# Keeping every engine's instructions in the order of the kernel's own plan

## The chip, the cores and the metric

The kernel runs on one core of a Trainium2 chip. The metric is the device time of one execution in microseconds (us); lower is better. A core has five engines with a queue of instructions each: TensorE (PE, with its weight loads shown apart as PEld), VectorE (DVE), ScalarE (ACT), GpSimd (POOL) and SyncE (SP), which here issues all transfers (DMAs). An engine starts its instructions in the order of its queue; an instruction whose operands aren't there yet waits, and so does all that stands behind it.

## The reference

One step of a decoder layer for 16 meta tokens, a prompt of 256 and 8 samples of 4 new tokens, 304 rows (T) in all, each 2048 wide, in fp32:

```python
xn = rms_norm(x, norm_mix)
z = xn @ w_in                                  # 2048 -> 7456 columns
o_a, S_a = rwkv7_mixer(z[..., :RWKV_COLS], ...)    # 16 heads of 64: a recurrence over tokens
o_b, S_b = retention_mixer(z[..., RWKV_COLS:], ...) # 4 heads of 256: rotary, masked scores, state
h = x + concatenate([o_a, o_b]) @ w_out
hn = rms_norm(h, norm_ffn)
h = h + (silu(hn @ w_gate) * (hn @ w_up)) @ w_down  # 2048 -> 5632 -> 2048
y = rms_norm(h, norm_final)
```

The kernel returns y, and the new states of both kinds of heads.

## The kernel before

**The main stream.** All large products have the activations transposed, 128 channels on the partitions and up to 304 tokens in the free dimension. Weights come from HBM in blocks of 128 x 1024 fp32 (`load`, buffers "wr", four of them). `halve` (L540) splits 512 columns into a rounded half "wh", by a cast on ACT (L545), and a rest "wl", by a subtraction on DVE (L546); four buffers of each. For every 128 x 128 piece TensorE then runs three matmuls (L584 to L586): rounded weights by rounded activations (xh), by the activations' rest (xl), and weights' rest by xh. 512 columns are thus a step of 12 matmuls. `main` (L552) goes through all jobs in a fixed sequence: 59 column tiles of the input projection ("in"), 32 of the output projection in two halves ("out"), then the FFN in groups of four gate and up tiles and 16 short "down" jobs. Results are summed in PSUM in two "acc" buffers, and each job's sum is taken out by an evacuation on DVE or ACT. At the start of each 512-column step `main` calls the load of a block up to 4096 columns ahead (L577) and the split of the weights that TensorE reads two steps later (L579, L580). In the first 16 pieces it also converts the input x to xh and xl as it arrives (`convert`, L576 and L582).

**The head streams.** Everything else runs beside it as generators: eight pairs of RWKV heads (`pair`, L817, with `inverse` at L1000, `sample`, and `units` at L1080), four retention heads (`ret`, L1291), small low-rank weights (`lora_weights`, L784), evacuations, norms. They use small fp32 matmuls in other PSUM tiles ("mm"), with DVE, ACT and GpSimd in between. `inverse` has a loop of 15 steps, each a shuffle on DVE (L1017), a product and a sum on GpSimd; later it copies products to a tile yy on ACT (L1064) between two sets of matmuls. `units` goes through five time units, each with four matmuls and an update of the state on DVE (L1114). `pair` begins with a scaled copy kk on ACT (L841). A pair may begin while the one before is still at work, so two pairs and a retention head are usually under way.

**The order.** The kernel plans its own order. Each engine handle is wrapped in `Timed`, and each call is first booked with estimated durations in the class `Plan`: for DVE 60 + 1.05 ns for each element of a row, for ACT 190 + 0.84, for GpSimd 100 + 2.2, and a latency (L336). TensorE is booked in `array`, SP not at all. `run` (L380) asks after each three matmuls of the main stream whether a generator is due on the estimated clock of TensorE; if so it lets it run to its next `yield`, and sets its next due time to the end of what it has just called, or 300 ns later if nothing was booked (L376). So the calls come in an order in which, by these estimates, everything is ready when its turn comes. The temporary tiles of the streams all lie in one large tile, "arena", whose places are assigned in a first pass of the same plan (the draft), and may be used again soon after.

The tile framework then makes five queues of these calls. [...]

Of the kernel before, what the change touches and what calls it, by code (L numbers as in the profile page):

```python
# [288 lines left out]
class Timed:  # L289


    def __init__(self, plan, eng, name):
        self._plan, self._eng, self._name = plan, eng, name

    def __getattr__(self, what):
        f = getattr(self._eng, what)

        def call(*a, **k):
            self._plan.book(self._name, what, a, k)
            return f(*a, **k)  # L300

        return call


class Plan:
# [1 line left out]

    def __init__(self, nc, rooms, draft):  # L310
        self.rooms, self.draft, self.count = rooms, draft, 0
        self.clock = dict(PE=0.0, DVE=0.0, ACT=0.0, POOL=0.0)
        self.ready = self.end = 0.0
        self.mode, self.parts, self.empty, self.begun = None, {}, 0.0, 0.0
        self.streams, self.made = [], 0
        self.pe = Timed(self, nc.tensor, "PE")
        self.dve = Timed(self, nc.vector, "DVE")
        self.act = Timed(self, nc.scalar, "ACT")
        self.pool = Timed(self, nc.gpsimd, "POOL")
        self.sp = Timed(self, nc.sync, "SP")  # L320
# [151 lines left out]
class Step:  # L472


    def __init__(self, tc, I, O, ctx, rooms, draft):
        self.tc, self.nc, self.I, self.O = tc, tc.nc, I, O
        self.rooms, self.draft = rooms, draft
        pool = lambda n, b, **k: ctx.enter_context(tc.tile_pool(name=n, bufs=b, **k))
        self.cp = pool("const", 1)
        self.wp = pool("weights", 1)  # L480
        self.mp = pool("scratch", 1)
        self.ap_ = pool("acc", ACC, space=bass.MemoryType.PSUM)
        self.pp = pool("psum", 8 - ACC, space=bass.MemoryType.PSUM)
        self.n = 0
        self.plan = pl = Plan(self.nc, rooms, draft)
        self.sp = pl.sp
        if not draft:
            self.arena = {dt: self.mp.tile([P, r.size], dt, tag=f"arena_{dt}", name=f"arena_{dt}")
                          for dt, r in rooms.items()}
        self.pe, self.dve, self.act, self.pool = pl.pe, pl.dve, pl.act, pl.pool  # L490
        self.outs = []
        self.live = 0
        self.done = set()
# [1182 lines left out]
```

## Time and profile before

| what | value |
|---|---|
| median of three runs (lowest, highest) | 1583.23 us (1579.57, 1583.24) |
| profiled execution | 1582.62 us |
| its span, first to last instruction | 1580.8 us |
| mean granted TensorE clock | 0.992 |
| busy, share of the span: PE / DVE / ACT / POOL | 98% / 71% / 53% / 12% |
| DMA, mean over the span | 160 GB/s, 252.50 MB |

Rows of the profile name an instruction by engine, operation and tiles: `mm<-arena_dt.float` is a matmul of a head stream, `acc<-xh,wh` one of the main stream, `arena_dt.float<-mm` takes a result of the first out of PSUM. All calls pass through the helper, so every row has line L300; the shape and the tiles tell which one it is. In the timeline the brackets give the idle time of the engine before an instruction, and what ended it. TensorE's matmuls overlap: one of 288 columns is shown with some 295 ns and starts about 133 ns after the one before.

### The profile page before, as it was taken

What the parts mean: (1) busy time and instruction counts of PE and PEld (TensorE: products, weight loads), DVE (VectorE), ACT (ScalarE), POOL (GpSimd) and SP (SyncE); (2) the same over time, 40 slices, a digit from 0 to 9 for tenths busy, and PEclk for the clock granted to TensorE, in tenths of its full rate; (3) what the DMA queues carried; (4) which work ended last, traced back from release to release, by engine and by line L of the source; (5) the groups of instructions that cost most, each with busy time, mean ns of one, the idle gap of its engine ahead of it and who ended that gap; (6) DMA issues with size and microseconds to landing.
All of it is one profiled execution on the core that took longest, in us unless ns stands there. A gap on an engine that the chain in (4) does not pass through costs nothing.

```text
span 1580.8 us, 30987 instructions
## 1 busy us (share of the span) xinstructions
PE 1544.1 (98%) x11388; PEld 1510.5 (96%) x11388; DVE 1125.7 (71%) x2590; ACT 842.7 (53%) x1795; POOL 182.5 (12%) x567
## 2 busy tenths in 40 slices
PE   9999999999999999999999999999999999999997
PEld 8989899998988989999999999999999999999997
DVE  7888789887997877776565656666666666565657
ACT  6756777577766556365444444444444444444445
POOL 1463314513143000000000000000000000000000
PEclk9999999999999999999999999999999999999999
DMA  7543344334544547755555555555555555555553
GB/s 280 152 126 108 102 121 138 118 102 126 181 131 139 168 161 231 241 162 160 166 167 165 169 163 171 162 171 161 169 165 166 168 163 171 162 172 162 169 163 114
DMA packets 77000, 252.50 MB, mean 160 GB/s; under 512 B 9392, under 2 KB 14640, under 8 KB 76848
## 3 DMA queue, kind: packets, MB, share of 16 engines
q1 hardware_dynamic: 76848, 250.52, 51.0%
q8 instruction: 90, 1.47, 0.4%
q14 instruction: 62, 0.51, 0.1%
HBM read 236.21 MB, written 14.28 MB: 158 GB/s over the span
## 4 chain that ended last, share of the span: by engine, by line
PE 68%; ACT 1%; DVE 1%; DMA 0%; issue 0%; POOL 0%; DVEq 0%; ACTq 0%; POOLq 0%
PE acc L300 64%; PE mm L300 4%; ACT arena_dt.float L300 1%; DVE arena_dt.float L300 1%; DMA arena_dt.float<-s0r 0%; DVE wl L300 0%; ACT wh L300 0%; ACT arena_dt.float32r L300 0%; POOL arena_dt.float L300 0%; DVEq L1672 0%; DVE arena_dt.float32r L300 0%; ACTq L300 0%; DVEq L300 0%; POOLq L300 0%
## 5 line engine op out<-in xcount | busy, mean ns | idle before, releaser
L300 ACT CAST wh<-wr 128x512 fp32r<-128x512 f32 x826 | 509.5, 619 | 577.4 <-PE acc L300 537.8
L300 PE MATMUL acc<-xh,wh 128*128 128x288 f32 (+2 forms) x2592 | 791.8, 305 | 0.5 <-ACT wh L300 0.3
L300 DVE TENSOR_TENSOR wl<-wr,wh 128x512 fp32r<-128x512 f32 x826 | 571.3, 693 | 282.2 <-ACT wh L300 259.9
L300 PE MATMUL acc<-xh,wl 128*128 128x288 f32 (+2 forms) x2592 | 771.3, 298 | 0.7 <-DVE wl L300 0.7
L300 PE MATMUL acc<-xl,wh 128*128 128x288 f32 (+2 forms) x2592 | 768.1, 296 | 0.0
L300 PEld LDWEIGHTS acc<-xh,wh 128*128 128x128 f32 x2592 | 488.3, 188 | 6.4 <-issue 2.7
L300 PEld LDWEIGHTS acc<-xl,wh 128*128 128x128 f32 x2592 | 487.5, 188 | 4.6 <-issue 1.4
L300 PEld LDWEIGHTS acc<-xh,wl 128*128 128x128 f32 x2592 | 486.9, 188 | 1.7 <-DVE wl L300 1.2
L300 PE MATMUL acc<-arena_dt.float32r,wh 128*128 128x288 f32 x1408 | 280.3, 295 | 0.0
L300 PEld LDWEIGHTS acc<-arena_dt.float32r,wh 128*128 128x128 f32 x1408 | 225.4, 188 | 0.3 <-ACT arena_dt.float32r L300 0.2
L300 PE MATMUL acc<-arena_dt.float32r,wl 128*128 128x288 f32 x704 | 206.8, 294 | 0.0
L300 PE MATMUL mm<-arena_dt.float 128*128 128x128 f32 (+8 forms) x1072 | 171.9, 320 | 19.3 <-DVE arena_dt.float L300 10.6
L300 PEld LDWEIGHTS mm<-arena_dt.float 128*128 128x128 f32 (+1 forms) x1072 | 140.2, 185 | 36.9 <-issue 10.5
L300 DVE TENSOR_TENSOR arena_dt.float<-arena_dt.float 128x288 f32<-128x288 f32 (+10 forms) x483 | 157.3, 351 | 11.1 <-ACT arena_dt.float L300 4.4
L300 DVE TENSOR_TENSOR arena_dt.float<-arena_dt.float,acc 128x288 f32<-128x288 f32 x208 | 94.3, 454 | 64.3 <-PE acc L300 63.8
L300 PEld LDWEIGHTS acc<-arena_dt.float32r,wl 128*128 128x128 f32 x704 | 132.8, 189 | 0.0
L300 ACT COPY arena_dt.float<-mm 64x64 f32<-64x64 f32 (+9 forms) x330 | 92.4, 287 | 53.0 <-PE mm L300 48.1
L300 ACT ACTIVATE arena_dt.float<-arena_dt.float 128x288 f32<-128x288 f32 (+6 forms) x200 | 85.3, 432 | 33.8 <-DVE arena_dt.float L300 28.0
L300 DVE TENSOR_TENSOR arena_dt.float<-acc,arena_dt.float 128x288 f32<-128x288 f32 (+4 forms) x181 | 72.9, 420 | 30.9 <-PE acc L300 30.4
L300 POOL TENSOR_TENSOR arena_dt.float<-arena_dt.float 128x70 f32<-128x70 f32 (+14 forms) x240 | 85.2, 356 | 62.0 <-DVE arena_dt.float L300 47.2
L300 POOL COPY arena_dt.float<-arena_dt.float 128x32 f32<-128x32 f32 (+5 forms) x123 | 43.9, 372 | 148.5 <-DVE arena_dt.float L300 81.6
L300 ACT COPY arena_dt.float<-arena_dt.float 64x320 f32<-64x320 f32 (+5 forms) x96 | 38.3, 412 | 16.5 <-POOL arena_dt.float L300 10.1
(64 smaller groups left out, 680.7 us busy)
## 6 DMA issues: line engine op xcount, KB each, us to landing
wr<-big SPq DMA_DIRECT2D x409, 512.0 KB, 3.5
arena_dt.float<-s0r SPq DMA_DIRECT2D x16, 512.0 KB, 4.5
out_rts<-arena_dt.float SPq DMA_DIRECT2D x16, 512.0 KB, 3.9
arena_dt.float<-xT SPq DMA_DIRECT2D x4, 576.0 KB, 5.1
out_y<-arena_dt.float SPq DMA_DIRECT2D x8, 288.0 KB, 2.2
arena_dt.float<-xT SPq DMA_DIRECT2D x7, 304.0 KB, 5.8
wr<-big SPq DMA_DIRECT2D x8, 256.0 KB, 5.6
arena_dt.float<-lora SPq DMA_DIRECT2D x16, 128.0 KB, 2.9
```

The source lines that it names most:

```text
L300: return f(*a, **k)
```

## The change

`Timed` hands each instruction that it made to a function `keep`, which the plan has been given:

```diff
         def call(*a, **k):
             self._plan.book(self._name, what, a, k)
-            return f(*a, **k)
+            return self._plan.keep(f(*a, **k))
...
-    def __init__(self, nc, rooms, draft):
+    def __init__(self, nc, rooms, draft, keep):
+        self.keep = keep
...
-        self.plan = pl = Plan(self.nc, rooms, draft)
+        self.plan = pl = Plan(self.nc, rooms, draft, (lambda i: i) if draft else tc.keep_in_program_order)
```

In the draft `keep` does nothing. In the real pass it is the framework's `keep_in_program_order`, which adds an edge from the instruction to the last one called on the same engine:

```python
prev = next((i for i in reversed(cur.bb.instructions)
             if i is not ins.ins and i.engine == engine), None)
if prev is not None:
    self.add_manual_dep(ins.ins, prev.name,
        mybir.DependencyInfo(mybir.DependencyClass.NoSync, mybir.DependencyReason.DATA), ...)
```

The edge is without a semaphore: it fixes the place in the queue and adds no wait for the end of the other instruction. All five queues then hold the calls in the plan's order, SP's transfers too. Instructions, operands, buffers and places in the arena stay as they are.

## The prediction

> **What bounds the kernel now.** I read the page first, then the windows, then TensorE's waits, then single stalls in the timeline. The page says that TensorE is the bound, and that what can change lies in the few per cent that it isn't busy:
>
> ```profile
> PE 1544.1 (98%) x11388; PEld 1510.5 (96%) x11388; DVE 1125.7 (71%) x2590; ACT 842.7 (53%) x1795; POOL 182.5 (12%) x567
> ...
> PE 68%; ACT 1%; DVE 1%; DMA 0%; issue 0%; POOL 0%; DVEq 0%; ACTq 0%; POOLq 0%
> ```
>
> The busy time by stage (columns: window, then busy us of PE, PEld, DVE, ACT, POOL, then the granted clock) says where that is:
>
> ```profile
> 20.00:640.00 620.00, 596.71 (x4268) 565.99 (x4267) 515.02 (x1517) 404.24 (x1032) 178.87 (x538) 0.99 0.46 145
> 640.00:1560.00 920.00, 919.78 (x6945) 918.94 (x6945) 583.86 (x1016) 416.25 (x723) 0.00 (x0) 1.00 0.55 167
> 1560.00:1581.00 21.00, 10.22 (x83) 9.89 (x81) 13.22 (x31) 6.14 (x12) 0.00 (x0) 0.82 0.29 114
> ```
>
> From 640 us on (output projection, FFN) PE has 0.22 us of idle in 920: nothing is to be gained there. From 20 to 640 us, where the head streams run beside the input projection, it is idle 620.00 - 596.71 = **23.3 us**. Its waits in that window (us, times, longest):
>
> ```profile
> PE mm L300 <- DVE arena_dt.float L300: 10.6, 9, 2.6
> PE mm L300 <- ACT arena_dt.float L300: 9.8, 5, 3.8
> PE acc L300 <- DVE wl L300: 0.7, 1, 0.7
> ```
>
> So about 20 us are 14 waits of a head stream's small matmul ("mm") for DVE or ACT; weights ("wl") make it wait once. After four of these waits TensorE also ran at half its clock:
>
> ```profile
> 119.36:126.19 6.83, 6.16 (x27) 6.19 (x28) 3.46 (x11) 2.11 (x5) 0.00 (x0) 0.50 0.31 91
> 310.51:313.92 3.41, 3.41 (x18) 3.41 (x16) 2.42 (x8) 1.70 (x4) 1.20 (x5) 0.50 0.04 14
> 368.53:371.95 3.42, 2.93 (x11) 2.57 (x12) 1.68 (x8) 1.41 (x6) 0.00 (x0) 0.50 0.53 146
> 505.07:508.48 3.41, 3.41 (x34) 1.39 (x32) 1.56 (x11) 0.07 (x1) 2.59 (x11) 0.50 0.21 79
> ```
>
> That is 17.07 us at 0.50, which cost half of it, **8.5 us**. All that a new order can give back between 20 and 640 us is thus 23.3 + 8.5 = 31.8 us.
>
> **Why those waits happen.** An instruction in the kernel as built keeps the number of its call, so the plan's order is known beside the order on the chip. TensorE has it nearly everywhere: 63 of its 10770 matmuls stand ahead of one called earlier. DVE has 713 such of 2470, ACT 562 of 1793, GpSimd 246 of 563, SP 66 of 523. Two stalls, on ACT and PE, then on DVE and PE:
>
> ```profile
> 113.58 1.05 PE L300 MATMUL mm<-arena_dt.float 128*128 128x128 f32 x8
> ...
> 114.53 1.13 ACT L300 CAST wh<-wr 128x512 fp32r<-128x512 f32 x2
> 118.69 0.56 ACT L300 ACTIVATE arena_dt.float<-arena_dt.float,pv 128x312 f32<-128x312 f32 x1 [3.03 <-POOL arena_dt.float L300]
> 119.15 0.73 ACT L300 COPY arena_dt.float<-mm 64x256 f32<-64x256 f32 x2
> ...
> 120.03 1.94 PE L300 MATMUL mm<-arena_dt.float 128*128 128x64 f32 x8 [3.80 <-ACT arena_dt.float L300]
> ```
>
> The two copies of `inverse` (L1064, calls 1543 and 1544) have had their matmuls since 114.63. Ahead of them in ACT's queue stands the `kk` of the next pair (L841, call 1687), which waits 3.03 us for GpSimd, and PE waits 3.80 for the copies. The plan has the copies first.
>
> ```profile
> 365.12 0.38 PE L300 MATMUL mm<-arena_dt.float 128*128 128x128 f32 x2
> ...
> 365.17 0.48 DVE L300 TENSOR_TENSOR arena_dt.float<-arena_dt.float,cst 128x256 f32<-128x256 f32 x1
> 367.78 0.01 DVE L300 LOAD_MASK_SELECT arena_dt.float<-arena_dt.float  x1 [2.12 <-POOL arena_dt.float L300]
> 367.78 0.24 DVE L300 STREAM_SHUFFLE arena_dt.float<-arena_dt.float 128x80 f32<-128x80 f32 x1
> 367.92 0.95 DVE L300 SCALAR_TENSOR_TENSOR arena_dt.float<-mm,arena_dt.float 128x288 f32<-128x288 f32 x3
> ...
> 369.02 0.77 PE L300 MATMUL mm<-arena_dt.float 128*128 128x128 f32 x2 [2.58 <-DVE arena_dt.float L300]
> ```
>
> The same on DVE: a shuffle of another pair (L1017, call 4926) waits for GpSimd, and the state updates of `units` (L1114, calls 4830 and 4831), whose matmuls ended at 365.5, stand behind it. In three more, a shuffle, a mask product or a state copy with a later number sits in front of what PE needs:
>
> ```profile
> 185.84 0.35 PE L300 MATMUL mm<-arena_dt.float 128*128 128x128 f32 x1 [2.65 <-DVE arena_dt.float L300]
> ...
> 309.51 0.68 PE L300 MATMUL mm<-arena_dt.float 128*128 128x128 f32 x4 [1.83 <-DVE arena_dt.float L300]
> ...
> 504.72 0.50 PE L300 MATMUL mm<-arena_dt.float 128*128 128x128 f32 x2 [2.28 <-ACT arena_dt.float L300]
> ```
>
> **The change, part by part.** Nothing is computed differently; five queues get the order of the calls.
>
> *DVE and ACT, 20 to 640 us.* The five stalls (3.80 + 2.58 + 2.65 + 1.83 + 2.28 = 13.1 us) go, since what blocked them moves behind. Of the other 23.3 - 13.1 = 10.2 us I take half, 5.1, because there the chain itself is partly late: -18.2 us (bounds 0 and -23.3). Of the half clock, which followed four of those five, I take 6.8 of 8.5, one stretch of 3.4 (1.7 lost) coming back.
>
> [...]
>
> *What is late next.* The planner's own durations (L336) are short in places, and its order is then a little early:
>
> ```profile
> L300 DVE SCALAR_TENSOR_TENSOR arena_dt.float<-mm,arena_dt.float 64x64 f32<-64x64 f32 x64 | 17.9, 280 | 2.6 <-PE mm L300 1.5
> ...
> L300 POOL COPY arena_dt.float<-arena_dt.float 128x32 f32<-128x32 f32 x56 | 21.9, 398 | 86.0 <-DVE arena_dt.float L300 73.7 <-PE mm L300 11.9
> ```
>
> It books 60 + 1.05 x 64 = 127 ns for the first, 280 in the trace: 64 x 0.153 = 9.8 us if each delays PE, nothing if the 0.4 us steps of the main stream (three matmuls, L584) hide it. Both orders pay this; I add 3, nearer to nothing, because the old order shows 2.6 us of idle before all 64 of them. Where a wait now heads a queue, whatever the plan put later stands behind it, weight casts first of all; DVE, 515.02 of 620 us busy, has 105 us for such waiting, and ACT 216. The plan calls a cast two 512-column steps before PE reads it, and in the old order "wl" made PE wait 0.7 us in all, so this cover holds; without it PE would pay each of these waits in full. A queue that waits at its head for TensorE costs nothing by itself: it has then done all that the plan put before, and PE is the one that is behind.
>
> *First 20 us.* The order puts each cast behind one more conversion of x (L582 stands before the next L580), 0.50 us by the row of two, and the conversion waits for its own DMA; the squares that ran at 9.64 go back to their place:
>
> ```profile
> 7.76 0.99 ACT L300 ACTIVATE xh<-arena_dt.float,pv 128x304 fp32r<-128x304 f32 x2 [0.19 <-DMA arena_dt.float<-xT]
> ...
> 9.64 1.21 ACT L300 ACTIVATE arena_dt.float<-arena_dt.float 128x1216 f32<-128x1216 f32 x1
> ```
>
> Between -0.7 and +1.5; I take +0.5, one conversion.
>
> *SP and GpSimd.* Loads of `s0`, `s0r`, `rmask`, `xT` that were drawn ahead go back between the weight loads; memsets go back into the streams. What might be late:
>
> ```profile
> ACT arena_dt.float32r L300 <- DMA arena_dt.float<-lora: 3.0, 5, 1.1
> ...
> ACT wh L300 <- DMA wr<-big: 1.7, 2, 1.3
> ```
> ```profile
> wr<-big SPq DMA_DIRECT2D x409, 512.0 KB, 3.5
> ...
> arena_dt.float<-lora SPq DMA_DIRECT2D x16, 128.0 KB, 2.9
> ```
> ```profile
> 0.97 3.40 POOL L300 MEMSET arena_dt.float<- 128x80 f32 x24
> ```
>
> Weights were waited for twice in the old order; four blocks of two steps each are in flight, which hides a load held up by a state load ahead of it. Were that cover gone, a block would cost its 3.5 us. I take 0 for SP, +1 for the `lora` copies (0 to 3.0 more), and 0 for GpSimd: 3.40 us of memsets move into the streams of an engine that is 178.87 of 620 us busy; uncovered they would cost those 3.4.
>
> *From 640 us on.* DVE already runs as planned here, an evacuation between two weight subtractions:
>
> ```profile
> 795.27 0.69 DVE L300 TENSOR_TENSOR wl<-wr,wh 128x512 fp32r<-128x512 f32 x1
> 796.29 0.46 DVE L300 TENSOR_TENSOR arena_dt.float<-arena_dt.float,acc 128x288 f32<-128x288 f32 x1 [0.33 <-PE acc L300]
> 796.87 0.69 DVE L300 TENSOR_TENSOR wl<-wr,wh 128x512 fp32r<-128x512 f32 x1
> ```
>
> In the gate and up columns the SiLU chain changes places with a weight subtraction (about one DVE instruction in eight), under four steps of TensorE work for each column. So zero here, and for the tail, whose last steps have the calls' order; with the cover gone a swap would cost the 0.69 of a subtraction.
>
> Sum: -18.2 - 6.8 + 3 + 0.5 + 1 = -20.5. The profiled execution took 1582.6 us (span 1580.8, 1.8 around it; 0.6 below the median of 1583.2): **1562 us**.
>
> **The rivals.** *Slower: the lora copy at the head of ACT.* `lora_weights` issues a DMA and, 300 ns of plan later (L371), calls ACT's copy of it. It lands 2.9 us after issue, 16 times. If SP gets to it no earlier than the plan, ACT stands 2.6 us each time with the streams' copies behind it, and PE waits as long: 16 x 2.6 = 42, so 1562 + 42 = 1604. It outweighs the gain from 20.5 / 16 = 1.3 us each. Against it: SP waits for little, so it issues ahead, and the row above has 3.0 us over all. 16%.
>
> *No difference.* Late chains make PE wait wherever the plan is short, and new waits eat the 20.5 us; or the pins change little that PE feels. 1578 to 1587, 10%.
>
> *Only the long stall frees the clock.* The three stretches beside shorter stalls come back wherever PE pauses: 3.4 us gained in place of 6.8, 1565.5. 8%, since three of the four stretches do stand beside stalls. [...]
>
> *More than the stalls.* PE's ends are modelled, and weight loading is idle 620 - 566 = 54 us where PE is idle 23.3; were all of that waiting, 30.7 more would come back: 1531. [...] But small matmuls outlast their weight load by shape, so 4%.
>
> **How the numbers follow.** The forecast holds 62%, 1551 (all 31.8 back) to 1577. 0.3% is 4.7 us, about what a measurement can tell from no change. Faster: 62 + 8 + 4 = 74%; same 10%; slower 16%. The range, 1551 to 1590, leaves out the 4% below and about 12 of the 16 above.
>
> **What would show it.** PE idle from 20 to 640 us below 12 us; none or one stretch at 0.50 between 20 us and the tail; no stall in which DVE or ACT waits for GpSimd while a result for PE stands ready; PE still full from the output projection on. Wrong, if ACT waits for `lora` sum to 20 us or more, if "wh" or "wl" appear among PE's waits with more than 5 us, or if stalls of `units` stay as they are: then the chains were late by themselves and the order wasn't the cause.

## The result, and the profile after

The changed kernel takes **1687.3 us** (median of 4 runs, 1683.9 to 1690.5) against 1583.2 before: a ratio of 1.0663, 95% interval 1.0637 to 1.0689, so 104 us slower. The prediction, 1562 us and "faster", had the wrong sign. The profiled execution took 1686.8 us with a span of 1685.0.

Busy times and the chain that ended last, from the page of the changed kernel:

```profile
PE 1577.3 (94%) x11388; PEld 1527.4 (91%) x11388; DVE 1123.4 (67%) x2590; ACT 820.7 (49%) x1795; POOL 161.2 (10%) x567
...
PE 64%; DVE 15%; ACT 7%; issue 6%; DMA 3%; POOL 2%; SPq 0%; DVEq 0%; POOLq 0%; ACTq 0%
```

The chain leaves TensorE for a third of the span, above all to VectorE and ScalarE. The page of before can't be set against this: its shares add up to only 70%, because its chain reaches back only to 453 us of the span and leaves out most of the stage with the head streams. The stages (windows of the changed kernel; columns as in the prediction) show where:

```profile
20.00:726.00 706.00, 627.41 (x4302) 584.52 (x4301) 521.78 (x1524) 395.49 (x1029) 160.65 (x562) 0.96 0.40 127
726.00:1646.00 920.00, 909.97 (x6831) 906.57 (x6829) 566.08 (x992) 394.46 (x705) 0.00 (x0) 1.00 0.55 167
```

The 4302 matmuls of the first window are about the 4268 that took 620 us before. Weight loading (PEld) is idle there for 706.00 - 584.52 = 121.5 us, before 620.00 - 565.99 = 54.0. In the second, the same 920 us hold 6831 matmuls instead of 6945. So some 80 us are lost beside the streams and 15 behind them, and the rest, some 9, in the last 39 us. Over the whole span PEld is idle for 1685.0 - 1527.4 = 157.6 us, before 1580.8 - 1510.5 = 70.3. That is 87.3 us of the 104.2; its busy time has grown by the other 16.9, all of it in the stretches at half clock (outside them it is 132 ns for each load in both kernels).

What TensorE waits for (20 to 726 us, changed kernel: us, times, longest):

```profile
PE mm L300 <- DVE arena_dt.float L300: 39.2, 29, 6.5
PE acc L300 <- ACT wh L300: 16.5, 6, 4.9
PE mm L300 <- POOL arena_dt.float L300: 7.4, 5, 2.3
PE mm L300 <- ACT arena_dt.float L300: 6.4, 5, 3.6
PE mm L300 <- DMA arena_dt.float<-s0r: 4.7, 6, 2.0
```

"wh", a cast weight of the main stream, made TensorE wait once before (20 to 640 us), for 0.3 us. Two of the three signs that the prediction named for being wrong are there: wh over 5 us, and ScalarE's waits for lora over 20. This is what ScalarE waited for in the kernel before (20 to 640 us):

```profile
ACT wh L300 <- PE acc L300: 68.6, 66, 4.2
ACT arena_dt.float L300 <- PE mm L300: 53.6, 60, 2.4
ACT arena_dt.float L300 <- DVE arena_dt.float L300: 43.1, 43, 3.4
ACT arena_dt.float L300 <- POOL arena_dt.float L300: 23.6, 16, 3.0
```

and in the changed one (20 to 726 us):

```profile
ACT arena_dt.float L300 <- PE mm L300: 98.4, 63, 4.9
ACT arena_dt.float L300 <- DVE arena_dt.float L300: 72.0, 50, 4.5
ACT arena_dt.float L300 <- POOL arena_dt.float L300: 48.0, 13, 6.9
ACT wh L300 <- PE acc L300: 31.1, 28, 2.7
ACT arena_dt.float32r L300 <- DMA arena_dt.float<-lora: 24.5, 10, 5.5
```

The line "wh <- PE acc" of before is the one to read twice. There the cast waits for a buffer that TensorE still reads: ScalarE cast as far ahead as four buffers allow. That line has halved, and the waits of stream instructions (the other three) have grown from 120.3 to 218.4 us, in a window 86 us longer. VectorE shows the other side; its wait for a cast was 33.6 us before, and in the changed kernel (20 to 726 us):

```profile
DVE wl L300 <- ACT wh L300: 115.2, 67, 6.4
```

One such place in the timeline of the changed kernel, all engines, 70 to 83 us (other rows left out):

```profile
70.55 1.64 ACT L300 CAST wh<-wr 128x512 fp32r<-128x512 f32 x3
...
74.99 2.49 POOL L300 COPY arena_dt.float<-arena_dt.float 128x32 f32<-128x32 f32 x9 [4.15 <-issue]
75.38 0.48 DVE L300 TENSOR_TENSOR arena_dt.float<-arena_dt.float 128x312 f32<-128x312 f32 x1
...
77.02 0.30 PE L300 MATMUL acc<-xh,wl 128*128 128x288 f32 x1
...
77.43 1.79 POOL L300 MEMSET arena_dt.float<- 128x256 f32 x6
...
79.06 2.34 ACT L300 COPY arena_dt.float<-arena_dt.float 128x32 f32<-128x32 f32 x7 [6.88 <-POOL arena_dt.float L300]
...
81.31 2.17 ACT L300 CAST wh<-wr 128x512 fp32r<-128x512 f32 x4
81.95 0.69 DVE L300 TENSOR_TENSOR wl<-wr,wh 128x512 fp32r<-128x512 f32 x1 [6.09 <-ACT wh L300]
81.97 0.61 PE L300 MATMUL acc<-xh,wh 128*128 128x288 f32 x1 [4.65 <-ACT wh L300]
```

The seven copies on ScalarE are those of `pair` (L911 to L917). They stand 6.88 us for GpSimd, which has nine copies and six memsets to do first and begins them only at 74.99. In the code all of these are in one step of the generator, and `book` (L338) lets every instruction of a step begin when the step is due, so the plan doesn't know that the copies need the memsets. Behind the copies stand four casts; VectorE stands 6.09 us for the first of them, with an evacuation behind; TensorE runs out of cast weights at 77.3 and stands 4.65. The granted clock is 0.50 from 80.2 us on:

```profile
80.20:87.00 6.80, 5.03 (x18) 4.63 (x19) 3.40 (x7) 4.17 (x9) 1.95 (x3) 0.50 0.48 140
```

There are ten of these between 20 us and the tail, 64.8 us together; before there were four with 17.07.

### The profile page after: what moved, and what is told of

Its sections match the earlier page's. It is cut to its first block, busy times and chain, and to the rows that moved or that the text cites. A ratio compares the mean times of both kernels' runs of the same rounds, so it can differ in the third digit from the quotient of the medians.

```text
span 1685.0 us, 30932 instructions
## 1 busy us (share of the span) xinstructions
PE 1577.3 (94%) x11388; PEld 1527.4 (91%) x11388; DVE 1123.4 (67%) x2590; ACT 820.7 (49%) x1795; POOL 161.2 (10%) x567
## 4 chain that ended last, share of the span: by engine, by line
PE 64%; DVE 15%; ACT 7%; issue 6%; DMA 3%; POOL 2%; SPq 0%; DVEq 0%; POOLq 0%; ACTq 0%
PE acc L300 58%; DVE arena_dt.float L300 10%; PE mm L300 6%; DVE wl L300 4%; ACT arena_dt.float L300 4%; ACT wh L300 2%; POOL arena_dt.float L300 2%; DMA arena_dt.float<-s0r 1%; DMA arena_dt.float<-lora 1%; DVE arena_dt.float32r L300 0%; DMA out_rts<-arena_dt.float 0%; DMA arena_dt.float<-xT 0%; ACT arena_dt.float32r L300 0%; DMA out_rws<-arena_dt.float 0%; DVE xl L300 0%
## 5 line engine op out<-in xcount | busy, mean ns | idle before, releaser
L300 PE MATMUL acc<-xh,wh 128*128 128x288 f32 (+2 forms) x2592 | 800.3, 309 | 20.3 <-ACT wh L300 16.5
L300 ACT CAST wh<-wr 128x512 fp32r<-128x512 f32 x826 | 499.7, 617 | 373.5 <-PE acc L300 341.4
L300 PEld LDWEIGHTS acc<-xh,wh 128*128 128x128 f32 x2592 | 494.6, 191 | 27.3 <-ACT wh L300 17.8
L300 PEld LDWEIGHTS acc<-xh,wl 128*128 128x128 f32 x2592 | 492.2, 190 | 7.4 <-DVE wl L300 6.8
L300 PEld LDWEIGHTS acc<-xl,wh 128*128 128x128 f32 x2592 | 493.3, 190 | 4.9 <-issue 1.7
L300 PEld LDWEIGHTS acc<-arena_dt.float32r,wh 128*128 128x128 f32 x1408 | 225.2, 188 | 14.8 <-issue 13.1
L300 PE MATMUL mm<-arena_dt.float 128*128 128x128 f32 (+8 forms) x1072 | 177.3, 319 | 48.6 <-DVE arena_dt.float L300 37.2
L300 DVE TENSOR_TENSOR arena_dt.float<-arena_dt.float 128x288 f32<-128x288 f32 (+12 forms) x483 | 158.0, 353 | 13.5 <-ACT arena_dt.float L300 8.3
L300 POOL TENSOR_TENSOR arena_dt.float<-arena_dt.float 128x5 f32<-128x5 f32 (+14 forms) x240 | 84.5, 353 | 159.8 <-DVE arena_dt.float L300 139.9
L300 ACT CAST arena_dt.float32r<-arena_dt.float 128x288 fp32r<-128x288 f32 (+4 forms) x73 | 30.5, 422 | 116.6 <-DVE arena_dt.float L300 92.0
```

The source lines that it names most:

```text
L300: return self._plan.keep(f(*a, **k))
```

## The experiments

A pin is the edge that `keep` adds. It adds no wait for the end of the other instruction: in the changed kernel a matmul of 288 columns, shown with 0.29 us, still starts 132 ns after the one before (median; the same in the kernel before). All runs are the changed kernel with something taken out of the pins, but for one ("More cover instead"), which changes four constants. Each ratio is to the kernel before, run beside it.

**One engine's pins at a time.** The helper of `Timed` pins only the engines named:

```diff
-            return self._plan.keep(f(*a, **k))
+            made = f(*a, **k)
+            return self._plan.keep(made) if self._name in ("ACT",) else made
```

ScalarE:

> Pins on ScalarE alone; the other four queues are free as before. Theory A (a wait at the head of ScalarE's queue holds up the weight casts behind it, and so the main stream): most of the 104 us come back here, 1640 to 1690 us, with ScalarE waiting for lora and GpSimd about 70 us between 20 us and the output projection as in the changed kernel. Theory B (it is VectorE's order): within 10 us of 1583. Theory D (one pinned queue is harmless, since the free ones make up for it; only queues pinned together that wait for each other cost the time): 1575 to 1600.

Measured 1582.6 us, ratio 0.9995 (0.9985 to 1.0005). VectorE:

> Pins on VectorE alone. Theory A (ScalarE's heads): within 15 us of 1583, and VectorE waits for wh about 34 us as before. Theory B (VectorE's order: a weight subtraction or an evacuation stands behind a step that waits for ScalarE or GpSimd): 1640 to 1690. Theory D (only queues pinned together): 1575 to 1600.

1579.8 us, 0.9982 (0.9973 to 0.9991). GpSimd and SyncE:

> Pins on GpSimd and on the DMA issues (SyncE) alone, the compute queues free. Theory C (loads and memsets that used to go ahead are now late: lora lands after its copy's turn, s0r after the state matmuls' turn): 1620 or more, with waits for lora of 20 us and more. Theories A, B and D: within 8 us of 1583, since a late load holds up only what needs it as long as the compute queues may pass it.

1597.2 us, 1.0080 (1.0063 to 1.0096). TensorE:

> Pins on TensorE alone, whose order has 63 inversions in 10770. All theories: little, 1575 to 1592. Only if TensorE's few inversions had filled long waits would it be 1600 or more.

1590.4 us, 1.0035 (1.0014 to 1.0056). Theories A and B fall: neither ScalarE nor VectorE costs anything alone. The four effects against the 1582.7 of the kernel before are -0.1, -2.9, +14.5 and +7.7, together 19 us; 85 of the 104 are made by pins together. GpSimd with SyncE costs more than any theory but C gave it, but C's own figures (1620, lora over 20 us) fail too. Note that ScalarE pinned alone does wait more at its head; rows of that run (20 to 640 us):

```profile
ACT arena_dt.float L300 <- PE mm L300: 78.4, 60, 4.8
ACT arena_dt.float L300 <- DVE arena_dt.float L300: 55.4, 38, 3.2
ACT wh L300 <- PE acc L300: 27.9, 30, 2.5
```

Against 53.6 and 43.1 before, the first two are 37 us more of waiting, for nothing lost. The third, the wait for a free weight buffer, has fallen from 68.6 as far as in the changed kernel (31.1), and the median time from the end of a cast to its first matmul is 4.33 us, against 4.50 there and 5.64 before. So the casts run ahead as little here as there, and that alone costs nothing. In this run, waits at the head of one queue are bearable while the other queues are without pins.

**Engines together.** The same edit with other names. ScalarE and VectorE:

> Pins on ScalarE and VectorE together, TensorE, GpSimd and SyncE free. Each alone gave 1582.6 and 1579.8. Theory D1 (the two fixed queues wait for each other in turn: the casts stand behind a step that waits for VectorE, and the subtractions behind one that waits for ScalarE): 1640 or more. Theory D2 (a fixed TensorE queue is needed too, since its main stream then stands behind a late small matmul): 1575 to 1600. Theory D3 (the loads in their planned place are what the fixed compute queues wait for): 1575 to 1600.

1637.1 us, 1.0357 (1.0336 to 1.0378). All but ScalarE:

> Everything pinned but ScalarE. TensorE alone gave +8, GpSimd with SyncE +14, VectorE -3, so by the sum of single effects 1602. Theory D1: 1595 to 1615, since a free ScalarE casts ahead. Theory D2: 1630 or more (fixed TensorE and VectorE). Theory D3: 1630 or more (fixed loads and VectorE).

1604.2 us, 1.0139 (1.0124 to 1.0154). All but VectorE:

> Everything pinned but VectorE. By the sum of single effects 1605. Theory D1: 1595 to 1615. Theory D2: 1630 or more (fixed TensorE and ScalarE). Theory D3: 1640 or more, with waits of ScalarE for lora of 20 us as in the changed kernel.

1618.9 us, 1.0234 (1.0217 to 1.0251). All but SyncE:

> Everything pinned but the DMA issues. Theory D3: 1583 to 1610, ScalarE's waits for lora back at some 3 us. Theories D1 and D2: 1660 to 1680, the 1687 less some 10 to 25 us for the waits for lora and s0r.

1672.2 us, 1.0574 (1.0558 to 1.0589). And ScalarE, VectorE and TensorE:

> ScalarE, VectorE and TensorE pinned, GpSimd and SyncE free. Tells how the 35 us between ScalarE with VectorE (1637) and all but SyncE (1672) divide. If a pinned TensorE makes late small matmuls stop the main stream: 1655 to 1670. If it is GpSimd's order that holds ScalarE up (its waits for GpSimd were 46 us there, 32 with GpSimd free): 1637 to 1650.

1654.3 us, 1.0453 (1.0427 to 1.0479). Of the three, D1 comes nearest, though the pair's run is 3 us under its bound and no_dve 4 us above its range: the pair costs 55.7 us where its members cost nothing, which D2 and D3 had put at 20 at most. The rest comes in steps: TensorE on top of the pair +17.2 (just under the forecast for it), GpSimd +17.9 (to 1672.2), SyncE +15.1 (to 1687.3). These are differences of medians from different rounds, in which the kernel before differed by up to 1.8 us. Either of the pair set free takes out 68 to 83 us of the whole. In the pair's own run (20 to 640 us), VectorE, ScalarE and TensorE:

```profile
DVE wl L300 <- ACT wh L300: 84.1, 63, 5.2
```
```profile
ACT arena_dt.float L300 <- DVE arena_dt.float L300: 77.9, 56, 4.5
```
```profile
PE acc L300 <- ACT wh L300: 9.7, 8, 3.6
```

The two queues stand for each other: ScalarE for a stream's result from VectorE with casts behind it, VectorE for one of these casts with the streams' next results behind it. Of 223 subtractions in this window 55 ended less than 0.3 us before TensorE first read them, against 4 of 239 in the kernel before (each matched with its matmul in the trace). This count doesn't measure the loss: with all five engines pinned, which is slower, it is 22 of 209.

**The casts out of the pins.** Both instructions of `halve` made without a pin:

```diff
-            return self._plan.keep(f(*a, **k))
+            made = f(*a, **k)
+            return self._plan.keep(made) if self._plan.pinned else made
...
+        self.plan.pinned = False
         self.act.copy(hi, raw)
         self.dve.tensor_sub(lo, raw, hi)
+        self.plan.pinned = True
```

With all five engines pinned otherwise:

> All five queues pinned, but the two instructions of halve (the cast wh on ScalarE, the subtraction wl on VectorE) are left out of the pins. Theory T2 (the casts, which the main stream needs every 1.6 us, stand behind streams' instructions that wait, and couple the two queues): most of the 104 us go, 1585 to 1615, and wh and wl leave TensorE's waits. Theory T1 (the streams' own chains are held up in the queues, casts or not, and the pinned TensorE stands for them): 1650 or more, with TensorE's waits for VectorE still near 39 us. In between, both.

1614.8 us, 1.0198 (1.0177 to 1.0218). With ScalarE and VectorE alone:

> ScalarE and VectorE pinned without the casts, the other queues free; with the casts this pair gave 1637. In that run 55 of 223 subtractions ended less than 0.3 us before TensorE read them, 4 of 239 in the kernel before. Theory T2: 1570 to 1590. Theory T1: 1615 or more.

1581.5 us, 0.9994 (0.9983 to 1.0005). With VectorE alone:

> VectorE alone pinned, without the subtractions. VectorE alone with them gave 1579.8 and showed 18 of 242 subtractions late by the 0.3 us measure. Theory T2: those go, 1570 to 1579, below both kernels. Theory T1: 1577 to 1583, no different from the pins with the subtractions.

1583.1 us, 0.9996 (0.9983 to 1.0010): T2 misses here, the subtractions out of the pins win nothing where VectorE alone is pinned. In the other two T2 holds, with 72 of 104 us and all of the pair's 55.7. Which of the two instructions it is, with one of them between the two lines at a time and all five engines pinned otherwise; the subtraction wl:

> Everything pinned but VectorE's subtractions wl; ScalarE's casts wh stay in their place. If VectorE's standing for wh (115 us in 67 waits in the changed kernel) is what makes the chains late: near 1615, as with both casts free. If the casts are already late on ScalarE, behind its own waits: 1660 or more, with wh still among TensorE's waits.

1693.0 us, 1.0687 (1.0665 to 1.0710), nothing gained. The cast wh:

> Everything pinned but ScalarE's casts wh; the subtractions stay in their place. If the casts are late on ScalarE behind its own waits: near 1615, and VectorE's waits for wh fall from 115 us to some 20. If it is VectorE's own place for wl: 1660 or more.

1612.7 us, 1.0183 (1.0161 to 1.0206). **It is ScalarE's casts**, 75 of the 104 us. But the subtraction out of its pin did not stop VectorE from standing; in that run (20 to 640 us):

```profile
DVE wl L300 <- ACT wh L300: 119.5, 73, 6.9
```

In this run the subtraction still has its place in VectorE's queue and waits there, so the run doesn't show that VectorE's standing is harmless, only that its pin isn't what makes it. With the casts wh free (20 to 640 us) ScalarE casts ahead again until no buffer is left, and TensorE has no wait for wh:

```profile
ACT wh L300 <- PE acc L300: 96.7, 98, 2.9
```
```profile
PE mm L300 <- DVE arena_dt.float L300: 10.6, 12, 4.4
PE mm L300 <- ACT arena_dt.float L300: 8.7, 7, 2.4
```

One reservation. The pin ties an instruction to the last call before it on its engine, whatever that is. A cast without a pin thus also loosens its neighbours: of ScalarE's 967 other calls 51 now stand ahead of an earlier one (before 256, in the changed kernel none). Casts free and all else strictly in order was not tried.

The casts free, and the DMA issues too:

> Everything pinned but the casts and the DMA issues; with the DMA issues pinned as well it was 1615. GpSimd and SyncE pinned alone gave +14, and all but SyncE 15 less than all. If these 14 are SyncE's: 1598 to 1603. If they are GpSimd's: 1610 or more.

1608.9 us, 1.0162 (1.0135 to 1.0190). The 5.9 us less than with them pinned are at the edge of the intervals; it is in the gap between both forecasts, and the rest of GpSimd with SyncE's 14 us isn't settled.

**ScalarE and VectorE pinned, only the casts wh free.**

> ScalarE and VectorE pinned, only ScalarE's casts wh left out; the subtractions keep their place. The pair with both casts in the pins gave 1637, with neither 1581.5. If the casts on ScalarE alone are the lock: 1572 to 1584, and where it is under 1579.8 it beats both kernels. If the subtractions matter as soon as the other queues are free: 1595 or more.

**1576.6 us, 0.9962 (0.9948 to 0.9976)**: 6.7 us below the kernel before in the same rounds, and the best of all. Its rows (20 to 640 us) for VectorE and ScalarE, against 84.1 and 77.9 above, for TensorE, and the window:

```profile
DVE wl L300 <- ACT wh L300: 7.8, 8, 2.9
```
```profile
ACT arena_dt.float L300 <- DVE arena_dt.float L300: 22.2, 29, 2.4
```
```profile
PE mm L300 <- ACT arena_dt.float L300: 5.6, 13, 0.7
PE mm L300 <- DVE arena_dt.float L300: 3.0, 7, 1.1
```
```profile
20.00:640.00 620.00, 603.72 (x4322) 568.55 (x4321) 522.24 (x1529) 401.85 (x1030) 176.90 (x538) 1.00 0.47 150
```

The waits of small matmuls for VectorE and ScalarE, 20.4 us before, are 8.6; none is over 1.1; and the granted clock is 1.00 (before 0.99). That is the mechanism that the prediction counted on, with the casts left out of it.

**More cover instead.** If the casts are only called too late, calling them earlier should do:

```diff
-LATE = 20000
+LATE = 4000
...
-WR = 4
+WR = 3
...
-WS = 4
+WS = 5
...
-ROOM = 33000
+ROOM = 33072
```

> All five queues pinned, with one more buffer for the cast weights, so that each cast is called three 512-column steps before TensorE reads it and not two; paid for with one raw weight buffer less and outputs issued 4 us of plan after they are made and not 20. If a cover of two steps is too short for ScalarE's waits (the casts late): 1620 to 1665, with TensorE's waits for wh under 8 us. If the casts' place in the queue costs through the streams' chains and not through the casts being late for TensorE: 1675 to 1695.

**1704.5 us**, 1.0765 (1.0747 to 1.0782): slower still, beyond both forecasts. The casts did come earlier: the median from the end of a cast to its first matmul went from 4.50 to 6.79 us (5.64 in the kernel before), and 11 of 208 subtractions instead of 22 of 209 were late by the measure above. But TensorE's waits for wh stay, 17.1 us (20 to 640 us, then a row of ScalarE's):

```profile
PE mm L300 <- DVE arena_dt.float L300: 31.4, 26, 3.5
PE mm L300 <- ACT arena_dt.float L300: 22.5, 11, 4.2
PE acc L300 <- ACT wh L300: 17.1, 4, 5.0
```
```profile
ACT arena_dt.float L300 <- POOL arena_dt.float L300: 55.4, 13, 7.6
```

A step is 1.6 us (12 matmuls at the 132 ns given above) and the waits at ScalarE's head reach 7.6 us in this run, so one step more doesn't outlast them; and a cast called earlier stands ahead of more stream work. So "two steps are too few" falls as the cause, as far as this run goes, which has one raw buffer less and earlier outputs as well.

**The pins in the FFN alone.** Everything pinned from the first result of the second half of the output projection on, nothing before:

```diff
-            return self._plan.keep(f(*a, **k))
+            made = f(*a, **k)
+            return self._plan.keep(made) if self._plan.pinned else made
...
             def f(acc):
+                if half and m == 0:
+                    self.plan.pinned = True
```

> Pins on all five engines, casts too, but only from the first result of the second half of the output projection on, after the streams have ended. The prediction said zero for this part; the changed kernel's windows lose about 1 us in 200 there and 4 to 5 in the last columns. 1585 to 1597 by these windows; 1581 to 1584 if that loss is only carried over from the mixed stage.

1603.1 us, 1.0123 (1.0098 to 1.0148), above both forecasts; its profiled execution, with a span of 1596.6, is its fastest. The loss is made here and isn't carried over. Part of it shows in the changed kernel's timeline, around the start of a block's "down" columns:

```profile
956.41 0.46 DVE L300 TENSOR_TENSOR arena_dt.float<-arena_dt.float 128x288 f32<-128x288 f32 x1
...
956.90 0.43 ACT L300 CAST arena_dt.float32r<-arena_dt.float 128x288 fp32r<-128x288 f32 x1 [2.03 <-DVE arena_dt.float L300]
...
957.24 1.14 ACT L300 CAST wh<-wr 128x512 fp32r<-128x512 f32 x2
...
957.89 0.69 DVE L300 TENSOR_TENSOR wl<-wr,wh 128x512 fp32r<-128x512 f32 x1 [1.02 <-ACT wh L300]
...
958.87 0.45 DVE L300 TENSOR_TENSOR arena_dt.float<-arena_dt.float,acc 128x288 f32<-128x288 f32 x1
...
959.46 0.50 PE L300 MATMUL acc<-arena_dt.float32r,wh 128*128 128x288 f32 x2 [0.38 <-DVE arena_dt.float L300]
```

It is the same loop in small. ScalarE's rounding of the activations stands 2.03 us for VectorE's product; two casts stand behind it; VectorE stands 1.02 us for a cast, with the evacuation of a short job behind; TensorE, which has only two "acc" buffers, stands for that. From one block's first down column to the next it is 76.83 us, before 76.19: some 6 us over all blocks. The larger part, some 10 us, comes in the last columns, from 1622 us on in the changed kernel (in pins_late likewise: the main stream's matmuls, paired by order with those of before, are 6.2 us late at 1534 us, and the span is 15.8 longer). There the same loop stands in nearly every step (changed kernel, 1620 to 1685 us):

```profile
ACT arena_dt.float L300 <- DVE arena_dt.float L300: 15.0, 16, 1.5
DVE wl L300 <- ACT wh L300: 16.0, 17, 1.1
```

With the casts wh free both losses are gone (free_wh is 31.2 us late from 820 us on and 31.3 at its last main-stream matmul); windows of free_wh and of the changed kernel:

```profile
1000.00:1200.00 200.00, 200.00 (x1514) 200.00 (x1513) 120.50 (x205) 88.31 (x149) 0.00 (x0) 1.00 0.53 166
```
```profile
1000.00:1200.00 200.00, 198.88 (x1500) 198.26 (x1499) 121.76 (x209) 83.56 (x147) 0.00 (x0) 1.00 0.54 166
```

## Why the prediction was wrong, step by step

**What bounds the kernel: right.** TensorE is the bound of the kernel before, and of the 31.8 us named as all that order can give back the best run gave 6.7.

**The five stalls go, -18.2, and the half clock, -6.8: the mechanism is right, with another set of pins.** In act_dve_wh the waits went as said and the granted clock rose from 0.99 to 1.00, but TensorE's idle time fell by 7.0 us (23.3 to 620.00 - 603.72 = 16.3), that of weight loading by 2.6 (54.0 to 51.4), and the span by 6.5 instead of 25: the 18.2 were mis-sized, as if nothing else were late where a stall goes. In the changed kernel those five stalls went too: before the same five matmuls (paired by tiles, shape and count) TensorE stands 0.0, 0.0, 0.7, 0.3 and 0.0 us, 1.1 in all and not 13.1. So this step was right there as well; others came, and the half clock with them (64.8 us of it between 20 us and the tail).

**The step that failed is "What is late next".** It says that what the plan put later stands behind a wait at the head of a queue, "weight casts first of all", and then books nothing for it, because VectorE has 105 us and ScalarE 216 free for waiting and because "wl" made TensorE wait 0.7 us in the old order, "so this cover holds". Three errors are in it. The one that costs: free time was taken engine by engine, but a wait on ScalarE becomes one on VectorE and comes back; the pair costs 55.7 us, its members nothing, and with the casts taken out of the pair's pins the 55.7 are gone. Then the 0.7 us were measured where casts ran ahead until no buffer was left (68.6 us of waiting for one), so they tell of four buffers of cover in the old order and not of two steps in the new; by itself this cost nothing, as act_only shows (TensorE's wait for wh is 4.9 us there). And the planner's error was looked for in durations (+3, L336), when what it leaves out is that one instruction of a step waits for another of the same step (L338). This last point is read from the code and from single places like the one at 79 us; no run with a mended plan was made.

**"A queue that waits at its head for TensorE costs nothing by itself": right as far as tested.** In act_only these waits grew from 53.6 to 78.4 us at no cost.

**First 20 us, +0.5: nothing to see.** PE is busy 16.99 us of them, before 17.38, but has 106 matmuls behind it and not 98.

**lora +1, SP 0, GpSimd 0: too low.** Both queues pinned alone cost 14.5 us. SyncE on top of all others costs 15.1, and 5.9 with the casts free. How the rest divides stays open, as does what makes GpSimd's 17.9 on top of ScalarE, VectorE and TensorE.

**TensorE's own pin, not costed:** 63 inversions in 10770 looked like nothing. It costs 7.7 alone and 17.2 on top of the pair, where a free TensorE had moved on with other work: its small matmuls' waits for VectorE were 6.0 us there, and are 31.4 with the pin.

**From 640 us on, zero, and for the tail: wrong.** Some 16 us in the changed kernel (6 in the blocks of the FFN, 10 in the last columns), 20 where this part alone is pinned. The rows quoted for it had one evacuation between two subtractions in a down block; the loop above sits where a down block begins, and in the last columns, which had been put at nothing because their order was the plan's already.

**The rivals.** The slower rival had the right place, the head of ScalarE's queue, with the streams' copies behind it, and its sign for it came (24.5 us for lora); but it made one wait of 2.6 us, 16 times, carry the whole, and got 1604. The lora waits are less than a tenth of ScalarE's, and most of the price is in the casts that stand behind all of them, which the rival didn't name. The other three rivals differ only in the size of the gain; none has a cost that comes from two queues at once, and so none could lead to 1687.

## What to carry to other kernels

Before you fix the order of several queues, look for the work that runs ahead today, here the line "wh <- PE acc", 68.6 us of waiting for a free buffer. With its place fixed it runs ahead less (27.9 us in act_only); that cost nothing while VectorE was free, and 55.7 us with VectorE fixed too. Slack could not be taken engine by engine here: two fixed queues that took turns waiting for each other cost 55.7 us and neither cost any alone, so try pins in pairs and leave out the prefetch. Here ScalarE and VectorE pinned without the weight casts gave 0.38% (0.24 to 0.52), VectorE pinned alone 0.18% (0.09 to 0.27), where all pins lost 6.6.

## What the hardware showed that I had not expected

**A third of the loss stands in TensorE's busy time.** PE's idle time, 1580.8 - 1544.1 = 36.7 us before and 1685.0 - 1577.3 = 107.7 after, explains 71 of the 104 us; the other 33 stand in its busy time, for the same 11388 matmuls. Weight loading's idle time explains 87 and leaves 17. So in this pair of traces the idle time of weight loading tells more of the loss. I had given that reading 4%, since small matmuls outlast their weight load (`mm<-arena_dt.float` in the kernel before: 320 ns against 185 in the mean), and used PE's idle time in the sum.

**Half clock stood beside a single pause of 1.71 us** (ws5, timeline and window):

```profile
415.39 0.33 PE L300 MATMUL mm<-cst,arena_dt.float 128*128 128x128 f32 x1 [1.71 <-POOL arena_dt.float L300]
```
```profile
416.20:419.60 3.40, 3.40 (x16) 3.40 (x15) 1.21 (x6) 3.33 (x13) 1.02 (x4) 0.50 0.08 31
```

In the kernel before, pauses of 1.83 us (up to 309.51) and 2.28 us (up to 504.72) had such a stretch behind them, from 310.51 and 505.07 on, and those of 2.65 us (up to 185.84) and 2.95 us (up to 461.98) had none; nor had one of 2.32 us in the changed kernel (up to 415.22). So in these runs a pause of 1.7 to 3 us may or may not have a stretch beside it, and I can't tell which from its length. Weight-load time grew by 16.9 us for 51.1 more us at half clock (64.8 and 12.8 in the tail, against 17.1 and 9.4), 0.33 for each and not the half that the prediction booked.
